# Seven products for the last column pairs of a down projection, on one core

## The chip, the cores and the metric

The kernel runs on one core of one Trainium2 chip. The metric is device time in microseconds (us): the median of three runs of the kernel before is 1959.01 us (1958.78 to 1959.5). One more execution was taken by the profiler; all lines of the profile and of the trace come from that one.

## The reference

The kernel computes an encoder trunk of two layers on 256 tokens of width 2048. Only the feed-forward part is touched by the change. Cut to that, the reference is:

```python
def conv_gated_ffn(h, w_up, conv_w, conv_b, w_down):
    a = depthwise_conv_centred(h @ w_up, conv_w, conv_b)
    g, u = jnp.split(a, 2, axis=-1)
    return (jax.nn.silu(g) * u) @ w_down
...
for l in range(DEPTH):
    ...                                   # norm, input projection, attention, gating, output projection
    x = x + conv_gated_ffn(rms_norm(x, norm2_g[l]), w_up[l], conv_w[l], conv_b[l], w_down[l])
```

`w_down[l]` has 5632 rows (44 row blocks of 128) and 2048 columns (4 column blocks of 512). The 256 tokens are two token blocks of 128, called m = 0 and m = 1.

## The kernel before

**Three products for one.** All arithmetic is float32 accurate, made from a faster format. Each operand is split into a high part (rounded, by ScalarE, here ACT) and a low part (the rest, a subtraction on VectorE, here DVE). A plain product of one row block, one column block and one token block takes three matmuls on TensorE (here PE): activation high with weight high, activation low with weight high, activation high with weight low. Each has a 128x128 stationary operand and 512 columns.

**Halves, pairs and pieces.** The feed-forward part runs in two halves of the hidden width: 20 row blocks, then 24 (`HALVES`). A half first makes its activations (`gate_and_up`, which fills `ys`), then multiplies them with `w_down`, in two groups ("pairs") of two column blocks: columns 0 and 1, then 2 and 3 (the loop over `group`, L1014). `down_blocks` lists the pieces of a pair in order. A plain piece is one column block with four row blocks (sometimes two): one load of 1 MB, one high part, one low part, 24 matmuls (`direct`, L221).

**Pieces by seven products.** Some pieces take two neighbouring row blocks and both column blocks of the pair, with the two token blocks: a 2x2 by 2x2 block product, which `seven` (L258) makes with seven products in place of eight, so with 21 matmuls in place of 24. It has a price on the other engines. DVE forms four sums of weight tiles (L268 to L270) in a second raw buffer, and both the weights (three tiles) and the sums (four tiles) are split (L264, L271, L272, L273). On the activation side `mixed` (L249) forms four sums of activation tiles on DVE and `parts` (L378) splits them; this is done once for a row pair and kept in `mixes`. Four extra accumulators take the shared products. When the pair's last such piece is done, `seven_out` (L308) adds them into the residual `xr` with one ACT copy and seven DVE operations, three of which (L318 to L320) have no urgency.

**Which pieces.** Before, `FAST` gives the first row block of each such pair of row blocks: three of ten in both pairs of the first half, four of twelve in the first pair of the second half, none in the second pair of the second half. There the order is by columns: all six pieces of column block 2, then all six of column block 3. `AFTER` says after how many plain pieces each stands.

**Buffers.** Raw weights have four buffers of 1 MB; a plain piece takes one, a piece by seven takes two. The high and low parts have three "wide" places each (`wide`, L149); a plain piece takes one, a piece by seven two. The input projections use the first two thirds of the same room as four "narrow" places of 1024 columns (`narrow`, L143). PSUM has three two-bank tiles `mm` and two one-bank tiles `tp`. A pair takes two `mm` for its sums, and with pieces by seven one more `mm` and both `tp`; in the very last pair of the last layer column block 3 has the two `tp` for its sums.

**Order.** Every engine's list is made by a scheduler from priorities: weight loads, splits and everything within `urgent()` come early, the rest fills in. `let_in` (L196), called in the middle of each piece, lets waiting steps in.

**Hand-over between layers.** When a column block c is finished in the first layer's second half, `done` adds it into `xr` (`residual`, L695), and `next_rows` (L651) makes the next layer's activations out of it: two ACT copies (L656), four transposing DMAs issued from SyncE (SP, L663), two ACT copies (L670) and four splits (L366 on ACT, L367 on DVE). The next layer's input projection reads them in order of c: it takes key block 0, 1, 2 (column blocks 0, 1, 2), then query block 0, then key block 3 (column block 3), each with 24 matmuls (L210, L215).

Of the kernel before, what the change touches and what calls it, by code (L numbers as in the profile page):

```python
# [15 lines left out]
P = 128  # L16
# [11 lines left out]
W = 512  # L28
KB = 4
# [4 lines left out]


HALVES = ((0, 20), (20, NF))
FAST = ((4, 8, 12), (4, 8, 12, 16))
AFTER = (2, 4, 5, 6)
PLACES = 6


def sevens(half, pair):

    return FAST[half] if half == 0 or pair == 0 else ()


def down_blocks(half, pair):

    f0, f1 = HALVES[half]
    c = (2 * pair, 2 * pair + 1)  # L50
    fast = sevens(half, pair)
    if not fast:
        return [((n,), tuple(range(k, min(k + KB, f1))), False) for n in c for k in range(f0, f1, KB)]
    plain = [k for k in range(f0, f1) if k - f0 - (k - f0) % 2 not in fast]
    own = [((n,), tuple(plain[i : i + KB]), False) for i in range(0, len(plain), KB) for n in c]
    for i, k in enumerate(fast):
        own.insert(AFTER[i] + i, (c, (f0 + k, f0 + k + 1), True))
    return own


# [7 lines left out]
def encoder(ctx: ExitStack, tc: tile.TileContext, xT, x, w_in, w_gu, w_o, w_up, w_down, wsT, pcol, prow, rope, out):  # L68
# [27 lines left out]
    def mm():  # L96
        return mmp.tile([P, 2, W], F32, tag="mm", name="mm")

    def tp(shape):
        return tpp.tile(shape, F32, tag="tp", name="tp")  # L100
# [603 lines left out]
    for l in range(DEPTH):  # L704
# [40 lines left out]
        for m in range(2):  # L745
            t = sl([P, W])
# [48 lines left out]
        for i in range(2):  # L795
# [5 lines left out]
            for m in range(2):  # L801
                t = row()
# [147 lines left out]
        def gate_and_up(j, ys, mixes):  # L950
            gs = []

            def gate_in(tall):
                for i in range(2):
                    g = together(tall[i])
                    y = convolved(g, 4 * j + 2 * i)
                    nc.scalar.activation(y, y, AF.Silu)
                    gs.append(y)

            def up_in(tall):  # L960
                for i in range(2):
                    u = together(tall[i])
                    y = gs[i]
                    t = convolved(u, NF + 4 * j + 2 * i)
                    nc.vector.tensor_tensor(out=y, in0=y, in1=t, op=ALU.mult)  # L965
                    for k in range(2):
                        ys.append(split_plain(y[:, k, :]))
                    k = len(ys) - 2
                    if k in FAST[half]:
                        e = mixed(y)  # L970
                        waiting.append(lambda e=e, k=k: mixes.__setitem__(k, parts(e, [P, W])))

            if j == 0:
                pss = [mm(), mm()]
                for b in range(NB):
                    for n in range(2):
                        up_rows(pss[n], n, j, b)
                        if b == NB - 1:
                            leave(pss[n], (gate_in, up_in)[n], 2)
                return  # L980
            for n in range(2):
                ps = mm()
                for b in range(NB):
                    up_rows(ps, n, j, b)
                leave(ps, (gate_in, up_in)[n], 2 + (j == f1 // 4 - 1))

        w_at = 0
        for half, (f0, f1) in enumerate(HALVES):
# [23 lines left out]
                        (nc.scalar if end and a else nc.sync).dma_start(out[:, m, c * W + a : c * W + a + step], to)  # L1012

            for group in range(2):  # L1014
                fast = sevens(half, group)
                blocks = down_blocks(half, group)
                sums, fresh = {}, {}
                n_fast = 0
                for n, (cs, ks, sevenfold) in enumerate(blocks):
                    end = last and not more and cs[0] == 3  # L1020
                    for c in cs:
                        if c not in sums:
                            t = None if end else mm()
                            sums[c] = [tp([P, W]) for _ in range(2)] if end else [t[:, m, :] for m in range(2)]
                            fresh[c] = set()
                    src = w_down[l, :, w_at : w_at + len(cs) * len(ks) * W]
                    w_at += len(cs) * len(ks) * W
                    acts = [ys[k - f0] for k in ks]
                    if sevenfold:
                        if n_fast == 0:  # L1030
                            t = mm()
                            extra = [t[:, 0, :], t[:, 1, :], tp([P, W]), tp([P, W])]
                        seven(
                            sums[cs[0]], sums[cs[1]], extra, acts, mixes[ks[0] - f0], src,
                            fresh[cs[0]], fresh[cs[1]], n_fast == 0, n_fast == len(fast) - 1,
                        )
                        n_fast += 1
                        if n_fast == len(fast):
                            seven_out(extra, cs[0])
                        continue  # L1040
                    c = cs[0]
                    finished = not any(c in b[0] for b in blocks[n + 1 :])
                    direct(sums[c], acts, src, fresh[c], finished, end and finished)
                    if finished:
                        done(c, sums[c], end)
# [71 lines left out]
```

## Time and profile before

| what | value |
| --- | --- |
| median of three runs | 1959.01 us |
| the profiled execution's own time | 1959.16 us |
| its span in the trace | 1957.4 us |
| time around the span | 1.76 us |
| granted TensorE clock over the span | 1.000 |
| matmuls | 8820 |
| weights read by the down projection in pieces of 1 MB / of 0.5 MB | 84 / 8 |

A stage in the trace is given by its start and end in us from the span's start. In this profile the start of a matmul in the chain that ended last lies some 0.16 us behind the start in the timeline; both are used as they stand. The layers' down projections lie here: first layer, first half 487.47 to 539.83 (columns 0 and 1) and 539.83 to 592.19 (columns 2 and 3); second half 853.31 to 915.87 and 915.87 to 981.15. Second layer: 1460.05 to 1512.41, 1512.41 to 1564.77, 1825.89 to 1888.45 and 1888.45 to 1953.74.

### The profile page before, as it was taken

The page shows a single profiled execution, that of the slowest core. Times are in us where ns is not written, and L with a number is a line of the kernel's source. Part 1 is how long each engine was busy: PE and PEld are TensorE (multiplying, and loading weights), DVE is VectorE, ACT ScalarE, POOL GpSimd, SP SyncE. Part 2 cuts the span into 40 slices and gives each one's busy share as a digit, 9 for nine tenths or more (in the row PEclk, how much of TensorE's full clock was granted, in tenths as well). Part 3 has the DMA queues.
Part 4 walks back from the last instruction along what each step waited for, and adds up shares of the span by engine and source line. Part 5 has one row for each costly group of instructions (what it writes and reads, how often), then busy time and mean ns, then how long its engine had stood idle before and what let it go on. Part 6 is the DMA issues. An engine that isn't in the chain of part 4 may idle for free.

```text
span 1957.4 us, 23117 instructions
## 1 busy us (share of the span) xinstructions
PE 1950.2 (100%) x8820; PEld 1619.1 (83%) x8820; DVE 1353.4 (69%) x1672; ACT 1326.1 (68%) x1461; POOL 21.3 (1%) x25
## 2 busy tenths in 40 slices
PE   9999999999999999999999999999999999999999
PEld 7888888888888888888888888888888888888887
DVE  5859775667875666678567796756669756666773
ACT  6776486777745777776566864877876556777742
POOL 0100000000000000000000000000000000000000
PEclk9999999999999999999999999999999999999999
DMA  9754586776566776657667446867765667677572
GB/s 360 217 199 151 195 256 192 218 226 215 185 219 219 222 222 214 221 164 269 196 202 249 143 163 213 247 199 223 227 212 186 220 212 228 210 224 225 163 269 85
DMA packets 191311, 414.04 MB, mean 212 GB/s; under 512 B 139488, under 2 KB 140768, under 8 KB 146656
## 3 DMA queue, kind: packets, MB, share of 16 engines
q1 hardware_dynamic: 190480, 411.83, 65.1%
q8 instruction: 69, 1.13, 0.2%
q10 hardware_dynamic: 720, 0.73, 0.1%
q14 instruction: 42, 0.34, 0.1%
HBM read 378.43 MB, written 2.10 MB: 194 GB/s over the span
## 4 chain that ended last, share of the span: by engine, by line
PE 97%; DMA 1%; DVE 1%; issue 0%; SPq 0%; ACT 0%; POOL 0%; DVEq 0%; ACTq 0%
PE mm L228 66%; PE mm L210 12%; PE mm L215 6%; PE mm L343 3%; PE tp L228 2%; PE mm L348 2%; PE mm L288 1%; PE mm L294 1%; PE mm L289 1%; DMA raw<-in_w_in 1%; DMA qk<-in_prow 1%; PE tp L289 0%; PE tp L294 0%; PE tp L288 0%; PE tp L386 0%; PE tp L616 0%
## 5 line engine op out<-in xcount | busy, mean ns | idle before, releaser
L156 DVE TENSOR_TENSOR los<-raw,his 128x2048 fp32r<-128x2048 f32 (+3 forms) x468 | 851.9, 1828 | 504.6 <-ACT his L182 362.5
L228 PE MATMUL mm<-his,sl 128*128 128x512 f32 x3808 | 902.4, 389 | 0.0
L228 PEld LDWEIGHTS mm<-his,sl 128*128 128x128 f32 x3808 | 715.0, 188 | 148.2
L182 ACT ACTIVATE his<-raw 128x2048 fp32r<-128x2048 f32 x248 | 466.8, 1883 | 182.9 <-PE mm L228 150.8
L228 PE MATMUL mm<-los,sl 128*128 128x512 f32 x1904 | 470.8, 389 | 0.0
L228 PEld LDWEIGHTS mm<-los,sl 128*128 128x128 f32 x1904 | 357.5, 188 | 74.1
L210 PE MATMUL mm<-his,sl 128*128 128x512 f32 x1152 | 311.0, 391 | 0.6 <-ACT his L171 0.5
L171 ACT ACTIVATE his<-raw 128x1024 fp32r<-128x1024 f32 (+1 forms) x180 | 186.0, 1039 | 158.5 <-PE mm L210 126.5
L210 PEld LDWEIGHTS mm<-his,sl 128*128 128x128 f32 x1152 | 215.1, 188 | 46.0 <-ACT his L171 0.9
L513 ACT COPY sl<-sl 128x1024 uint16<-128x1024 uint16 x98 | 132.3, 1350 | 112.8 <-DMA sl<-sl 112.8
L215 PE MATMUL mm<-los,sl 128*128 128x512 f32 x576 | 178.3, 390 | 1.2 <-DVE los L156 1.2
L215 PEld LDWEIGHTS mm<-los,sl 128*128 128x128 f32 x576 | 107.9, 188 | 24.3 <-DVE los L156 2.0
L916 ACT ACTIVATE sl<-sl,pc 128x256 f32<-128x256 f32 x176 | 95.3, 589 | 0.9
L937 ACT COPY sl<-sl 128x1024 uint16<-128x1024 uint16 x88 | 92.1, 1046 | 2.7
L917 DVE SCALAR_TENSOR_TENSOR sl<-sl,pc 128x255 f32<-128x255 f32 x176 | 77.4, 479 | 4.7 <-ACT sl L916 4.2
L920 DVE SCALAR_TENSOR_TENSOR sl<-sl,pc 128x255 f32<-128x255 f32 x176 | 77.4, 478 | 0.1
L374 ACT ACTIVATE sl<-sl 128x256 fp32r<-128x256 f32 x88 | 31.8, 408 | 66.1 <-DVE sl L965 66.1
L935 ACT ACTIVATE sl<-mm,yr 128x512 f32<-128x512 f32 x88 | 59.7, 679 | 4.9 <-PE mm L228 4.9
L343 PE MATMUL mm<-sl,his 128*128 128x512 f32 x256 | 62.1, 392 | 0.0
L271 ACT ACTIVATE his<-raw 128x2048 fp32r<-128x2048 f32 x20 | 38.3, 1913 | 28.6 <-DVE raw L270 26.6
L343 PEld LDWEIGHTS mm<-sl,his 128*128 128x128 f32 x256 | 47.1, 188 | 9.1
L367 DVE SCALAR_TENSOR_TENSOR sl<-sl,pc 128x256 fp32r<-128x256 f32 x96 | 42.2, 480 | 11.1 <-ACT sl L366 11.0
(145 smaller groups left out, 1167.5 us busy)
## 6 DMA issues: line engine op xcount, KB each, us to landing
raw<-in_w_up SPq DMA_DIRECT2D x176, 1024.0 KB, 5.0
raw<-in_w_down SPq DMA_DIRECT2D x84, 1024.0 KB, 4.6
raw<-in_w_in SPq DMA_DIRECT2D x38, 1024.0 KB, 5.0
raw<-in_w_o SPq DMA_DIRECT2D x32, 1024.0 KB, 4.9
raw<-in_w_gu SPq DMA_DIRECT2D x16, 1024.0 KB, 5.5
raw<-in_w_down SPq DMA_DIRECT2D x8, 512.0 KB, 3.3
sl<-sl SPq DMA_TRANSPOSE x244, 4.1
sl<-in_prow SPq DMA_DIRECT2D x12, 256.0 KB, 7.6
```

The lines of the kernel that those rows point to most:

```text
L156: nc.vector.tensor_tensor(out=lo, in0=part, in1=hi.bitcast(F32), op=ALU.subtract)
L171: nc.scalar.activation(hi[:, cs], part, AF.Copy)
L182: nc.scalar.activation(hi[:, :n], raw[:, :n], AF.Copy)
L210: nc.tensor.matmul(ps[m], acts[kk][:, part, m * P : (m + 1) * P], hi, start=first and kk == 0 and part == 0, stop=False,)
L215: nc.tensor.matmul(ps[m], acts[kk][:, 0, m * P : (m + 1) * P], lo, start=False, stop=last and kk == KB - 1)
L228: nc.tensor.matmul(ps[m], acts[kk][:, part % 2, m * P : (m + 1) * P], w, start=first, stop=done and kk == len(acts) - 1 and part == 2,)
L343: nc.tensor.matmul(ps[:, i, :], part_of(0, k, i), x1, start=k == 0, stop=False)
L513: nc.scalar.copy(words, tall.rearrange("p (b a) n -> p b (a n)", b=2))
L916: nc.scalar.activation(t[:, i, :], s[:, i, :], AF.Identity, bias=col(3), scale=col(1))
L917: nc.vector.scalar_tensor_tensor(out=t[:, i, 1:], in0=s[:, i, : SEQ - 1], scalar=col(0), in1=t[:, i, 1:], op0=ALU.mult, op1=ALU.add)
L920: nc.vector.scalar_tensor_tensor(out=t[:, i, : SEQ - 1], in0=s[:, i, 1:], scalar=col(2), in1=t[:, i, : SEQ - 1], op0=ALU.mult, op1=ALU.add)
L937: nc.scalar.copy(h, rows.bitcast(U16).rearrange("p (j n b) -> p j b n", j=2, b=2))
```

## The change

`FAST` and `AFTER` are given for each half and each pair. The second half's second pair now has four row pairs of twelve by seven products, placed as in its first pair; the first half's second pair has four of ten, one after each of the first four plain pieces. Its plain pieces are then six of four row blocks, where there were six of four and two of two. The row pair at block 16 of the first half gets its mixed activations, which it had not before. In the very last pair the four extra accumulators are two `mm` tiles, since column block 3 holds the two `tp`. The plain pieces of columns 2 and 3 in the second half now alternate, so that column block 2 ends one piece before column block 3. The weights are packed on the host in the new order of pieces.

```diff
 HALVES = ((0, 20), (20, NF))
-FAST = ((4, 8, 12), (4, 8, 12, 16))
-AFTER = (2, 4, 5, 6)
+FAST = (((4, 8, 12), (4, 8, 12, 16)), ((4, 8, 12, 16), (4, 8, 12, 16)))
+AFTER = (((2, 4, 5), (1, 2, 3, 4)), ((2, 4, 5, 6), (2, 4, 5, 6)))
...
-def sevens(half, pair):
-
-    return FAST[half] if half == 0 or pair == 0 else ()
...
-    fast = sevens(half, pair)
-    if not fast:
-        return [((n,), tuple(range(k, min(k + KB, f1))), False) for n in c for k in range(f0, f1, KB)]
+    fast = FAST[half][pair]
     plain = [k for k in range(f0, f1) if k - f0 - (k - f0) % 2 not in fast]
     own = [((n,), tuple(plain[i : i + KB]), False) for i in range(0, len(plain), KB) for n in c]
     for i, k in enumerate(fast):
-        own.insert(AFTER[i] + i, (c, (f0 + k, f0 + k + 1), True))
+        own.insert(AFTER[half][pair][i] + i, (c, (f0 + k, f0 + k + 1), True))
     return own
...
-                    if k in FAST[half]:
+                    if k in FAST[half][0] + FAST[half][1]:
                         e = mixed(y)
...
-                fast = sevens(half, group)
+                fast = FAST[half][group]
...
                         if n_fast == 0:
                             t = mm()
-                            extra = [t[:, 0, :], t[:, 1, :], tp([P, W]), tp([P, W])]
+                            extra = [t[:, 0, :], t[:, 1, :]]
+                            if last and not more and group:
+                                t = mm()
+                                extra += [t[:, 0, :], t[:, 1, :]]
+                            else:
+                                extra += [tp([P, W]), tp([P, W])]
```

## The prediction

> **What bounds the kernel now.** I read the page's first and fourth part, then the list of waits for PE, then the chain that ended last in order of time.
>
> ```profile
> span 1957.4 us, 23117 instructions
> PE 1950.2 (100%) x8820; PEld 1619.1 (83%) x8820; DVE 1353.4 (69%) x1672; ACT 1326.1 (68%) x1461; POOL 21.3 (1%) x25
> ...
> PE 97%; DMA 1%; DVE 1%; issue 0%; SPq 0%; ACT 0%; POOL 0%; DVEq 0%; ACTq 0%
> ```
>
> The chain is PE work for 97% of the span. A busy PE is no proof of a full one, so the waits come next (engine and line that waited, whom for: us in total, times, longest).
>
> ```profile
> PE mm L215 <- DVE los L156: 1.2, 1, 1.2
> PE tp L124 <- DVE ones L120: 1.1, 1, 1.1
> PE tp L616 <- DVE sl L608: 0.5, 1, 0.5
> PE mm L210 <- ACT his L171: 0.5, 1, 0.5
> ```
>
> That is the whole list: 3.3 us, none of it on a line of the down projection (L228 and L288 to L294). The chain gives the pace (start, length, matmuls).
>
> ```profile
> 269.87 228.48 PE mm L228 x1008
> ...
> 884.59 5.44 PE mm L228 x24
> 894.79 5.44 PE mm L228 x24
> 904.99 76.16 PE mm L228 x336
> ...
> 1877.57 43.52 PE mm L228 x192
> 1921.09 32.65 PE tp L228 x144
> ```
>
> 228.48 / 1008 = 0.22667 us a matmul. The same pace stands in 5.44 / 24 and 76.16 / 336. Between the two pieces of 24 lies a piece by seven: 894.79 - 884.59 - 5.44 = 4.76 us, and 21 x 0.22667 = 4.76. So a piece by seven runs at the plain pace too, and is 0.68 us shorter than the 24 matmuls that it replaces, with no wait before, in or behind it. PE is the bound here, and matmuls taken away come off the end one for one, as long as the others keep up.
>
> **The change part by part.** *Matmuls removed.* In a layer the first half's second pair goes from 231 to 228 (one more piece by seven), the second half's second pair from 288 to 276 (four more). That is 15 a layer, 30 in all: 30 x 0.22667 = **6.80 us**. The removed matmuls lie in the four stages that follow (the stage, then its length, busy us and number of instructions of PE, PEld, DVE, ACT, POOL, the granted clock, the DMA share, GB/s); the third row is the second half's first pair, which already has four of twelve.
>
> ```profile
> 487.47:539.83 52.36, 52.36 (x232) 43.37 (x232) 46.27 (x52) 37.71 (x37) 0.00 (x0) 1.00 0.56 194
> 539.83:592.19 52.36, 52.36 (x232) 43.37 (x232) 42.01 (x34) 24.35 (x16) 0.00 (x0) 1.00 0.62 218
> 853.31:915.87 62.56, 62.56 (x277) 51.82 (x277) 54.71 (x56) 43.67 (x39) 0.00 (x0) 1.00 0.64 227
> 915.87:981.15 65.28, 65.28 (x289) 54.07 (x289) 34.00 (x30) 43.72 (x50) 0.00 (x0) 1.00 0.63 206
> 1888.45:1953.74 65.29, 65.28 (x289) 53.73 (x287) 26.48 (x16) 17.40 (x10) 0.00 (x0) 1.00 0.38 132
> ```
>
> Here a rule speaks about the size of the gain. The Trainium skill, "TensorE: Matmul & The Clock Gate", section "Back-to-back issue gap", gives about 131 ns as the sustained spacing of 512-column matmuls in a real kernel, and N/2.4 + 2.5 ns, some 216 ns, for an isolated warm one. As estimates from that page the sum would be 30 x 0.131 = 3.9 us or 30 x 0.216 = 6.5 us. This trace has neither (0.22667 us over 1008 in a row), and the row decides.
>
> *DVE work added.* The prices (busy us, mean ns of one):
>
> ```profile
> L156 DVE TENSOR_TENSOR los<-raw,his 128x2048 fp32r<-128x2048 f32 x12 | 27.4, 2289 | 7.7 <-ACT his L271 7.2 <-ACT his L182 0.5
> L156 DVE TENSOR_TENSOR los<-raw,his 128x1536 fp32r<-128x1536 f32 x4 | 7.0, 1754 | 2.6 <-PE mm L228 2.6
> L268 DVE TENSOR_TENSOR raw<-raw 128x1024 f32<-128x1024 f32 x3 | 3.7, 1222 | 0.0
> ...
> L269 DVE TENSOR_TENSOR raw<-raw 128x512 f32<-128x512 f32 x3 | 2.1, 685 | 0.0
> ...
> L320 DVE TENSOR_TENSOR xr<-xr,sl 128x1024 f32<-128x1024 f32 x1 | 1.2, 1214 | 0.0
> ```
>
> A plain piece costs DVE 2.29 us, one by seven 1.22 + 2 x 0.69 + 1.75 + 2.29 = 6.64, so 4.35 more. `seven_out` is six operations of L269's size and one L320: 6 x 0.69 + 1.21 = 5.3. For the first layer's last pair that makes 34.00 + 4 x 4.35 + 5.3 = 56.7 us in a stage of 65.28 - 2.72 = 62.56, a share of 91%; for the second layer's 26.48 + 22.7 = 49.2, 79%. In the first half's second pair one piece by seven stands for two half pieces: at most 42.01 + 6.64 = 48.7 in 51.68, 94%, less what the two half pieces cost. The stages that run without a wait today have 54.71 / 62.56 = 87% and 46.27 / 52.36 = 88%. So DVE stays under PE in each stage, but with little left. I take 0, and keep 0 to 2 us in all for sevens whose low parts come late by the bunching of this work. ACT has more room:
>
> ```profile
> L264 ACT ACTIVATE his<-raw 128x1536 fp32r<-128x1536 f32 x20 | 29.8, 1489 | 19.3 <-PE mm L228 12.2 <-PE mm L289 7.0
> ```
>
> A piece by seven splits three tiles more than a plain one, 1.49 us; four make 43.72 + 6.0 = 49.7 of 62.56 in the first layer's last pair, 79%. Cost 0.
>
> *The mixed activations of block 16 in the first half* are new:
>
> ```profile
> L253 DVE TENSOR_TENSOR sl<-sl 128x256 f32<-128x256 f32 x14 | 5.9, 418 | 0.0
> L254 DVE TENSOR_TENSOR sl<-sl 128x128 f32<-128x128 f32 x14 | 4.1, 292 | 0.5
> L381 DVE TENSOR_TENSOR sl<-sl 128x512 fp32r<-128x512 f32 (+1 forms) x28 | 18.1, 652 | 25.2 <-ACT sl L380 25.2
> ```
>
> 0.42 + 2 x 0.29 + 0.65 = 1.65 us of DVE, in the stage of 46.27, which goes to 47.9 of 52.36. They are read only in the next stage. Cost 0, cover: those 4.5 us.
>
> *The first piece by seven of the first half's second pair* comes one plain piece earlier, and after a pair's end, where DVE also adds the sums into `xr`:
>
> ```profile
> 545.64 1.92 ACT L271 ACTIVATE his<-raw 128x2048 fp32r<-128x2048 f32 x1 [5.14 <-DVE raw L270]
> ...
> 550.71 0.23 PE mm L288
> ```
>
> Today its sums are split from 545.64 to 547.56. It would start at 550.71 - 5.44 = 545.27 and needs them nine matmuls in, at 547.31. Kept at its present time the split would hold PE for 0.25 us; but the second plain piece's low part now comes behind it in the order, which gives back up to 2.29 us. I take 0, bounds 0 to 0.3 in each layer.
>
> *Loads.* Eight half loads turn into four whole ones, the bytes are the same. A piece by seven holds two of four raw buffers; the alternation of the third stage row does so already without a wait. I take 0.
>
> *The hand-over between the layers* is the step without a direct row. Column block 2 used to end 32.64 us before column block 3, now 5.44. Call the end of column block 3 E. The next layer needs block 2's first activations behind two key blocks, at E + 2 x 24 x 0.22667 = E + 10.88. What the chain behind a finished column block takes, from the addition to the first split activation, is bounded by three pairs of rows, an L695 and an L367 (of whose two or four operations the first is ready some 0.45 us in):
>
> ```profile
> 912.81 0.68 DVE L318 TENSOR_TENSOR xr<-xr,sl 128x512 f32<-128x512 f32 x1
> ...
> 914.02 1.28 DVE L695 TENSOR_TENSOR xr<-mm,xr 128x512 f32<-128x512 f32 x2
> ...
> 929.57 1.67 DVE L367 SCALAR_TENSOR_TENSOR sl<-sl,pc 128x256 fp32r<-128x256 f32 x4
> ...
> 948.54 1.29 DVE L695 TENSOR_TENSOR xr<-mm,xr 128x512 f32<-128x512 f32 x2 [3.01 <-PE mm L228]
> ...
> 956.75 0.89 DVE L367 SCALAR_TENSOR_TENSOR sl<-sl,pc 128x256 fp32r<-128x256 f32 x2
> ...
> 981.48 1.28 DVE L695 TENSOR_TENSOR xr<-mm,xr 128x512 f32<-128x512 f32 x2
> ...
> 992.16 0.88 DVE L367 SCALAR_TENSOR_TENSOR sl<-sl,pc 128x256 fp32r<-128x256 f32 x2 [0.91 <-ACT sl L366]
> ```
>
> Block 2 today takes 956.75 + 0.45 - 948.54 = 8.7 us, block 3 11.1, block 0, which today stands just as block 2 will (after a `seven_out`, one piece before its neighbour), 16.0. When the addition can start is the second unknown. Block 0 ended at 904.99 + 5.44 = 910.43 and was added only from 914.02, 3.6 us later, because L318 and L319, without urgency, waited behind low parts; block 3, with no `seven_out` before it, 0.3 later. So block 2's first activations come between E - 5.1 + 8.7 = E + 3.6 and E - 1.9 + 16.0 = E + 14.1, and the wait is 0 to 3.2 us. The nearest row for the chain is block 3's 11.1, the same engines at the same place, and with the late start it gives E + 9.2: in time by 1.7 us. Block 0's 16.0 had no date to keep. I take 0. On SP the two sets of four transposes now stand 5.4 us apart:
>
> ```profile
> 984.34 5.23 SPq L663 DMA_TRANSPOSE sl<-sl  x4
> ```
>
> During each, SP issues no load for 5.2 us, and PE lives on the pieces already loaded; blocks 0 and 1 did the same to the pair behind them, without a wait. Block 3's own activations are due at E + 21.8; with 2.7 for the start and 16.0 for the chain they come at 18.7.
>
> *The end.* Block 2 of the last layer is written out one piece before the end, not six; nothing follows that would fill DVE, so I take 0 (0 to 0.6).
>
> **The sum** is 6.80: span 1957.4 to 1950.6. The profiled execution took 1959.16, so 1.76 lies around the span, and 0.15 over the median of 1959.01. Against the median the forecast is **1952.2 us**.
>
> **The rivals.** *The hand-over waits.* Block 2's chain goes like block 0's: PE waits at key block 2, up to 3.2 us once. For it: block 0 stands the same way; against it: block 3's chain beside the same input projection. Time 1952.5 to 1955.4. *DVE falls behind* in the dense stages: up to 2 us, 1952.5 to 1954.5, for it the 91%, against it that 87% and 88% run with no wait at all. *Slower than before:* the transposes of block 2 stand in SP's list behind a weight load that waits for a raw buffer.
>
> ```profile
> SPq L164 <- DVE los L156: 376.8, 73, 17.6
> ```
>
> SP has waited up to 17.6 us at such a load. Behind that one, activations due at E + 10.9 come at E + 9.2 + 17.6 = 26.8: a wait of 15.9, 9.1 over the gain, 1968.1 us. It decides from a wait of 6.8 on, and shows as slower from 10.7. Against it: the mean of those 73 waits is 5.2 us, which with 1.7 us of room leaves 3.5. The Trainium skill, the same page, section "What's actually happening", halves PE's clock after an idle window of about 3.4 us; by it such a wait would also cost some matmuls double. No wait here is that long (the list above), and every stage row has the clock at 1.00, so no run shows it. *A removed matmul gives back less than its pace*, as by the spacing of 131 ns in that page: 3.9 us, 1955.1; the rows speak against it. That the pieces by seven are not made is out: the lists are plain.
>
> **How the numbers follow.** Forecast without new waits 55%; hand-over 27%, of which 4 with more than 2.9 us; DVE late 9%, of which 2 come together with a hand-over wait and pass 2.9; SP's order 4%, of which 3 past 10.7 us; the smaller gain 1%; 4% for a better time by up to 1.3 us, since a new order also moves the 3.3 us of waits elsewhere. About 0.2%, 3.9 us, is what a measurement here tells from no change: faster means below 1955.1. Faster 55 + 23 + 7 + 4 = 89%, within 4 + 2 + 1 + 1 = 8%, slower 3%. The range is 1951.2 to 1955.5: below, part of the better case; above, the whole of the hand-over's bound.
>
> **What would show it.** Right: the chain shows all thirty pieces by seven of the two layers at 4.76 us; 8790 matmuls; no wait of PE between 487 and 592 or 853 and 1010. The hand-over wrong: PE waits on L366 or L367 at key block 2, some 10.9 us behind the last L228 of the first layer. DVE wrong: PE waits on L156 at L294. SP wrong: L663 stands behind a long wait of L164. The forecast is wrong, too, if attention in the second layer, where PE waits a little already, is ordered anew.

## The result, and the profile after

| | median, us | lowest to highest | runs |
| --- | --- | --- | --- |
| before | 1959.05 | 1958.78 to 1960.86 | 8 |
| after | 1954.23 | 1953.08 to 1956.62 | 8 |

The ratio is 0.9975, with a 95% interval of 0.9964 to 0.9986. The change makes the kernel faster by 4.8 us, of the 6.8 that were forecast. The forecast of 1952.2 is 2.0 too low, and the time lies inside the range.

In the changed kernel the lines behind `sevens` stand seven lower: L228 is now L221 (plain matmuls), L288 to L294 are L281 to L287 (pieces by seven), L268 to L270 are L261 to L263 (sums of weight tiles), L271 is L264 (high part of the sums), L210 and L215 are L203 and L208 (input projection), L171 and L182 are L164 and L175 (high parts of its weights and of plain pieces), L156 is L149 (low parts), L695 is L688 (addition), L663 and L670 are L656 and L663 (transposes, and the copies behind them), L366 and L367 are L359 and L360 (first split activations). L426 are the squares of a finished column block. Some experiments have one or two lines more: in e6 and e10, for example, the addition is L689.

These lines of the page of the kernel after answer to those shown of before: the span, the busy times, the chain by engine.

```profile
span 1953.7 us, 23130 instructions
...
PE 1946.0 (100%) x8790; PEld 1614.0 (83%) x8790; DVE 1404.9 (72%) x1732; ACT 1340.8 (69%) x1473; POOL 21.3 (1%) x25
...
PE 97%; DVE 1%; ACT 0%; issue 0%; POOL 0%; DVEq 0%
```

There are 8790 matmuls, 30 fewer, and PE is still the bound. The list of waits for PE has one entry that was not there before:

```profile
PE mm L203 <- DVE sl L360: 1.4, 2, 1.2
```

It is two waits. The long one, 1.15 us, ends at 30.11 us, in the start of the program, which the change doesn't touch (e1 comes back to it). The short one, 0.24 us, ends at 991.38, at key block 2 of the second layer.

To see what the change gave, I cut the run by the chain that ended last. Its longest pieces begin at fixed places of the program: the 1008 matmuls begin with the first half's up projection, the 1248 with the last 48 matmuls ahead of the second half's. After:

```profile
271.83 228.48 PE mm L221 x1008
...
582.91 282.88 PE mm L221 x1248
...
1242.07 228.48 PE mm L221 x1008
...
1553.16 282.88 PE mm L221 x1248
...
1944.85 5.45 PE tp L221 x24
```

Before, those not shown yet:

```profile
581.31 282.88 PE mm L228 x1248
...
1242.45 228.48 PE mm L228 x1008
...
1553.89 282.88 PE mm L228 x1248
```

| stretch (start to start) | before | removed, x 0.22667 | would be | after | lost |
| --- | --- | --- | --- | --- | --- |
| start to first up projection | 269.87 | 0 | | 271.83 | (see e1) |
| first half, layer 1 | 311.44 | 3: 0.68 | 310.76 | 311.08 | 0.32 |
| second half, hand-over, attention | 661.14 | 12: 2.72 | 658.42 | 659.16 | 0.74 |
| first half, layer 2 | 311.44 | 3: 0.68 | 310.76 | 311.09 | 0.33 |
| second half, layer 2, to the last matmul | 399.85 | 12: 2.72 | 397.13 | 397.14 | 0.01 |
| first up projection to last matmul | 1683.87 | 6.80 | 1677.07 | 1678.47 | 1.40 |

The last row is the work that the change touches: 5.40 us less, 1.40 lost, in two places. The first is the hand-over. Here the chain itself leaves PE (start, length, what):

```profile
986.38 0.43 PE mm L208 x2
986.81 0.70 ACT sl L426 x3
987.52 1.24 ACT sl L663
988.75 0.93 ACT his L164
...
989.71 1.23 DVE los L149
990.93 0.41 DVE sl L360
...
991.38 0.97 PE mm L203 x3
```

The chain before the change was all matmuls at this place. Now it goes through ACT: two squares of another block (L426), the copy behind a transpose (L663), a split of a weight, a low part, and only then the activation that PE waits for. With E the end of column block 3 (980.03), the first L360 is done at 991.28, E + 11.25, and it was due at about E + 10.88. The list's 0.24 us are only a part of what this costs. By the starts of successive matmuls PE loses 0.40 us at the one that waits for the first L360 and 0.11 at the next, and 0.23 more twelve matmuls on, at the second L360: 0.74, all that the stretch lost.

The second place is the last piece by seven of the first half's first pair, whose matmuls the change doesn't touch. Timeline after (start, length, engine and line, in brackets the idle time before):

```profile
521.58 0.75 DVE L368 TENSOR_TENSOR sl<-sl 128x256 fp32r<-128x256 f32 x2
522.25 0.69 DVE L374 TENSOR_TENSOR sl<-sl 128x512 fp32r<-128x512 f32 x1
522.85 0.69 DVE L262 TENSOR_TENSOR raw<-raw 128x512 f32<-128x512 f32 x1
523.46 1.75 DVE L149 TENSOR_TENSOR los<-raw,his 128x1536 fp32r<-128x1536 f32 x1
...
524.43 1.92 ACT L175 ACTIVATE his<-raw 128x2048 fp32r<-128x2048 f32 x1 [2.61 <-issue]
525.12 0.69 DVE L263 TENSOR_TENSOR raw<-raw 128x512 f32<-128x512 f32 x1
...
526.25 1.90 ACT L264 ACTIVATE his<-raw 128x2048 fp32r<-128x2048 f32 x1
...
527.35 0.84 PE L287 MATMUL mm<-los,sl 128*128 128x512 f32 x3
...
528.20 0.50 PE L281 MATMUL mm<-his,sl 128*128 128x512 f32 x1
```

Ahead of the sums L262 and L263 DVE splits activations (L368) and a mixed activation (L374). L263 ends late, at 525.81, and by then ACT is splitting a plain piece (L175, to 526.35), so that L264 starts only at 526.25. In the kernel before, in e4 and in e5 that plain split stands behind the split of the sums. L264 ends at 528.15, and PE's tenth matmul starts at 528.20, not at 527.35 + 3 x 0.22667 = 528.03. The list of waits doesn't have this one. It shows only in the starts of successive matmuls, 0.17 late here and 0.11 more at the next (528.54).

### The profile page after: what moved, and what is told of

Same layout as the page of the kernel before. It is cut to its first block, busy times and chain, and to the rows that moved or that the text cites. A ratio compares the mean times of both kernels' runs of the same rounds, so it can differ in the third digit from the quotient of the medians.

```text
span 1953.7 us, 23130 instructions
## 1 busy us (share of the span) xinstructions
PE 1946.0 (100%) x8790; PEld 1614.0 (83%) x8790; DVE 1404.9 (72%) x1732; ACT 1340.8 (69%) x1473; POOL 21.3 (1%) x25
## 4 chain that ended last, share of the span: by engine, by line
PE 97%; DVE 1%; ACT 0%; issue 0%; POOL 0%; DVEq 0%
PE mm L221 64%; PE mm L203 12%; PE mm L208 6%; PE mm L336 3%; PE mm L281 2%; PE mm L282 2%; PE mm L287 2%; PE mm L341 2%; PE tp L221 1%; PE tp L287 1%; PE tp L282 1%; PE tp L281 1%; PE tp L379 0%; PE tp L609 0%; PE tp L380 0%; PE tp L381 0%
## 5 line engine op out<-in xcount | busy, mean ns | idle before, releaser
L149 DVE TENSOR_TENSOR los<-raw,his 128x2048 fp32r<-128x2048 f32 (+3 forms) x476 | 867.6, 1833 | 466.3 <-ACT his L175 321.4
L221 PE MATMUL mm<-his,sl 128*128 128x512 f32 x3680 | 872.1, 389 | 0.0
L221 PEld LDWEIGHTS mm<-his,sl 128*128 128x128 f32 x3680 | 690.9, 188 | 143.2
L175 ACT ACTIVATE his<-raw 128x2048 fp32r<-128x2048 f32 (+1 forms) x236 | 446.8, 1895 | 123.0 <-PE mm L221 97.5
L221 PE MATMUL mm<-los,sl 128*128 128x512 f32 x1840 | 454.7, 389 | 0.0
L221 PEld LDWEIGHTS mm<-los,sl 128*128 128x128 f32 x1840 | 345.5, 188 | 71.6
L203 PE MATMUL mm<-his,sl 128*128 128x512 f32 x1152 | 312.2, 392 | 1.4 <-DVE sl L360 1.4
L164 ACT ACTIVATE his<-raw 128x1024 fp32r<-128x1024 f32 (+1 forms) x180 | 186.2, 1039 | 146.7 <-PE mm L203 125.5
L203 PEld LDWEIGHTS mm<-his,sl 128*128 128x128 f32 x1152 | 215.4, 188 | 47.7 <-DVE sl L360 2.9
L208 PE MATMUL mm<-los,sl 128*128 128x512 f32 x576 | 178.4, 390 | 1.2 <-DVE los L149 1.2
L208 PEld LDWEIGHTS mm<-los,sl 128*128 128x128 f32 x576 | 107.9, 188 | 24.4 <-DVE los L149 2.0
L264 ACT ACTIVATE his<-raw 128x2048 fp32r<-128x2048 f32 x30 | 57.4, 1914 | 63.9 <-DVE raw L263 38.6
L367 ACT ACTIVATE sl<-sl 128x256 fp32r<-128x256 f32 x88 | 31.9, 409 | 70.4 <-DVE sl L958 70.4
L257 ACT ACTIVATE his<-raw 128x1536 fp32r<-128x1536 f32 x30 | 44.6, 1487 | 28.7 <-PE mm L221 19.1
L281 PE MATMUL mm<-his,sl 128*128 128x512 f32 x154 | 60.1, 390 | 0.0
```

What stands on the lines that cost most here:

```text
L149: nc.vector.tensor_tensor(out=lo, in0=part, in1=hi.bitcast(F32), op=ALU.subtract)
L164: nc.scalar.activation(hi[:, cs], part, AF.Copy)
L175: nc.scalar.activation(hi[:, :n], raw[:, :n], AF.Copy)
L203: nc.tensor.matmul(ps[m], acts[kk][:, part, m * P : (m + 1) * P], hi, start=first and kk == 0 and part == 0, stop=False,)
L208: nc.tensor.matmul(ps[m], acts[kk][:, 0, m * P : (m + 1) * P], lo, start=False, stop=last and kk == KB - 1)
L221: nc.tensor.matmul(ps[m], acts[kk][:, part % 2, m * P : (m + 1) * P], w, start=first, stop=done and kk == len(acts) - 1 and part == 2,)
```

## The experiments

The same kernel's time differs by 3.5 us from run to run (the table above), more than most parts of this question are worth. So each experiment is read by the stretches of its trace as in the table; e1 shows how well these repeat. "Full" is the third column of numbers: 310.76, 658.42, 310.76, 397.13.

| run | median, us | ratio to before, interval | first half 1 | second half to next | first half 2 | second half 2 | sum |
| --- | --- | --- | --- | --- | --- | --- | --- |
| e1_again | 1953.68 | 0.9974 [0.9964, 0.9985] | 311.07 | 659.11 | 311.08 | 397.13 | 1678.39 |
| e2_only_second | 1954.49 | 0.9976 [0.9967, 0.9986] | 311.44 | 659.50 | 311.44 | 397.13 | 1679.51 |
| e3_only_first | 1958.28 | 0.9996 [0.9987, 1.0005] | 311.09 | 661.10 | 311.10 | 399.85 | 1683.14 |
| e8_order_alone | 1959.7 | 1.0002 [0.9993, 1.001] | 311.44 | 661.06 | 311.44 | 399.85 | 1683.79 |
| e4_early_mix | 1953.16 | 0.9972 [0.9961, 0.9982] | 311.05 | 659.14 | 311.03 | 397.14 | 1678.36 |
| e5_raw5 | 1952.97 | 0.997 [0.9958, 0.9981] | 310.76 | 659.15 | 310.76 | 397.13 | 1677.80 |
| e10_lo_later | 1955.17 | 0.9981 [0.9972, 0.999] | 311.59 | 659.18 | 311.59 | 397.13 | 1679.49 |
| e6_urgent_out | 1954.2 | 0.9975 [0.9966, 0.9984] | 311.60 | 659.12 | 311.51 | 397.15 | 1679.38 |
| e7_col2_earlier | 1952.68 | 0.9969 [0.9957, 0.998] | 311.16 | 658.41 | 311.08 | 397.13 | 1677.78 |
| e9_squares_dve | 1953.5 | 0.9972 [0.9961, 0.9982] | 311.13 | 658.41 | 311.10 | 397.13 | 1677.77 |
| e11_both | 1952.69 | 0.9969 [0.9957, 0.9981] | 310.76 | 658.35 | 310.76 | 397.12 | 1676.99 |
| e12_more | 1951.95 | 0.9965 [0.9952, 0.9977] | 310.08 | 658.37 | 310.08 | 397.13 | 1675.66 |

### e1: the changed kernel once more

No edit.

> The changed kernel once more, to separate what the change does from what a run does. The measure is the stretch from the first matmul of the first layer's up projection to the last matmul: 1683.87 us before, 1678.47 in the changed kernel's profile, 5.40 less (6.80 for 30 matmuls, less waits of some 0.33 in each layer's first half and 0.74 around the hand-over). Theory A (the first 272 us differ from run to run, whatever the change): the stretch is again 1678.5 within 0.2, and the start of the up projection lies anywhere from 269.9 to 272. Theory B (the change makes the start late): it starts at 271.8 again, within 0.2, in this and every other variant, and the kernel before stays near 269.9.

The four stretches repeat within 0.05 us. What doesn't repeat is the start: the first up projection begins at 269.88 us here, at 271.83 in the first trace, with the same program. One DVE operation near the start, first in e1:

```profile
25.95 0.17 DVE L473 TENSOR_SCALAR nsink<-qk 128x8 f32<-128x8 f32 x1 [3.63 <-DMA qk<-in_prow]
```

and the same one, with what follows it, in the first trace of the changed kernel:

```profile
28.33 0.17 DVE L473 TENSOR_SCALAR nsink<-qk 128x8 f32<-128x8 f32 x1 [5.70 <-DMA qk<-in_prow]
...
29.58 0.48 DVE L360 SCALAR_TENSOR_TENSOR sl<-sl,pc 128x256 fp32r<-128x256 f32 x1
...
30.11 0.98 PE L203 MATMUL mm<-his,sl 128*128 128x512 f32 x3 [1.15 <-DVE sl L360]
```

DVE's list holds a small operation (L473) that waits for a load of 132 KB, and the activation for which PE waits (L360) stands behind it. In the first trace the load landed 2.4 us later than in e1, and PE stood still. This is also the 1.2 us in the list of waits above. So the traced run of the changed kernel shows 1.95 us more than e1 for a reason that has nothing to do with the change.

### e2, e3, e8: the parts one by one

e2 keeps the first half as before and makes only the second half's second pair by sevens; e3 does the opposite; e8 makes no new piece by seven and only alternates the plain pieces of columns 2 and 3.

```diff
 # e2
-FAST = (((4, 8, 12), (4, 8, 12, 16)), ((4, 8, 12, 16), (4, 8, 12, 16)))
-AFTER = (((2, 4, 5), (1, 2, 3, 4)), ((2, 4, 5, 6), (2, 4, 5, 6)))
+FAST = (((4, 8, 12), (4, 8, 12)), ((4, 8, 12, 16), (4, 8, 12, 16)))
+AFTER = (((2, 4, 5), (2, 4, 5)), ((2, 4, 5, 6), (2, 4, 5, 6)))
 # e3 (with the old order by columns where there are no sevens)
+FAST = (((4, 8, 12), (4, 8, 12, 16)), ((4, 8, 12, 16), ()))
 # e8
+FAST = (((4, 8, 12), (4, 8, 12)), ((4, 8, 12, 16), ()))
```

> Only the second half's second pair by seven products; the first half as before. 24 matmuls less, 5.44 us. Theory A (the wait of 0.33 in each layer's first half comes from the new mixed activations of block 16, and the 0.74 from the hand-over): stretch 1683.87 - 5.44 + 0.7 = 1679.1, no wait in the first half, the hand-over wait as in the changed kernel. Theory C (the first-half wait comes from something else in the new order): the first half is 0.3 longer here too, stretch 1679.8.

> Only the first half's second pair with four of ten; the second half's second pair plain and by columns as before. 6 matmuls less, 1.36 us. Theory A: less two waits of 0.33: stretch 1683.87 - 1.36 + 0.66 = 1683.2, no wait at the hand-over. If the 0.74 is not of the hand-over but of a shifted schedule in the second layer, it is here as well: 1683.9.

> The kernel before with one thing of the change: the plain pieces of the second half's second pair alternate between columns 2 and 3, with no piece by seven there. Same matmuls as before. Theory A (order and seven_out make the hand-over late together): without a seven_out block 2 is added at once, some 5.1 us before the layer's end, and its first activations come with 8.7 to 11.1 us of chain at 3.6 to 6.0 us behind the end, due at 10.9: no wait, 661.1 us. Rival (the nearness of the two hand-overs alone does it): 661.8.

The parts add up but for one thing. e2 saves 1683.87 - 1679.51 = 4.36, e3 0.73, together 5.09; the whole saves 5.40 to 5.48. The rest of 0.3 to 0.4 is lost in e2's attention of the second layer, where its chain goes through a transfer that the chains before, after and of e1 don't have:

```profile
1091.14 6.61 DMA sl<-sl
```

The stretches tell more: the first half loses its 0.3 us only with the first half's part of the change (e1, e3), and the hand-over its 0.7 only with the second half's (e1, e2). e8 loses nothing: alternating the columns brings column block 2's end to 5.44 us before E, and the next layer still comes in time. With no `seven_out` ahead of it block 2 is added at E - 5.1 there, and the first L360 is done at E + 9.0, 1.8 us before its date. e8 beside before also says that the order by itself is worth nothing (1.0002 [0.9993, 1.001]).

### e4, e5, e10: what holds the first half

The suspects are the mixed activations of block 16 on DVE, the four raw buffers, and the order of DVE's list. e4 takes another row pair, block 2 in place of 16, whose activations are made earlier. e5 has a fifth raw buffer (with two small slots fewer, to have the room). e10 puts the low part of the three weight tiles behind the last sum.

```diff
 # e4
-FAST = (((4, 8, 12), (4, 8, 12, 16)), ...
+FAST = (((4, 8, 12), (2, 4, 8, 12)), ...
 # e5
-    slots = pool("slots", 54)
-    rawp = pool("rawp", 4)
+    slots = pool("slots", 52)
+    rawp = pool("rawp", 5)
 # e10
-            lo_part(lo[:, : 3 * W], raw[:, : 3 * W], hi[:, : 3 * W])
+            with tc.issue_after(latest(nc.vector.engine)):
+                lo_part(lo[:, : 3 * W], raw[:, : 3 * W], hi[:, : 3 * W])
```

> As the changed kernel, but the fourth row pair of the first half's second pair starts at block 2 instead of block 16, so that its mixed activations are made during the up projection and not in the crowded stage behind it. Same 30 matmuls less. Theory A: the first half's first pair is back at 52.36 us in both layers, stretch 1678.47 - 0.66 = 1677.8. Rival (the last piece by seven of the first pair waits because of the denser order behind it, whatever is mixed): the wait of 0.3 stays, stretch 1678.5.

In e4 the wait at the first pair's last piece by seven is gone, so the mixed activations in that stage brought it there. But the first half is as long as it was (311.05 against 311.08): the loss now stands at the *second* pair's last piece. The mixing decided where the time is lost, not whether. Timeline of e4:

```profile
578.59 4.49 DVE L149 TENSOR_TENSOR los<-raw,his 128x2048 fp32r<-128x2048 f32 x2 [2.06 <-ACT his L264]
...
580.93 0.50 PE L287 MATMUL mm<-los,sl 128*128 128x512 f32 x1
```

PE's L287 needs the low part of the sums, the first of the two L149, done at 578.59 + 2.29 = 580.88. The bracket tells why it is late: DVE stood still for 2.06 us until ACT had split the sums. The same stillness is in each turn of plain piece and piece by seven. One turn of DVE in the changed kernel:

```profile
561.88 1.22 DVE L261 TENSOR_TENSOR raw<-raw 128x1024 f32<-128x1024 f32 x1
563.01 1.75 DVE L149 TENSOR_TENSOR los<-raw,his 128x1536 fp32r<-128x1536 f32 x1
564.68 0.68 DVE L262 TENSOR_TENSOR raw<-raw 128x512 f32<-128x512 f32 x1
565.40 0.69 DVE L263 TENSOR_TENSOR raw<-raw 128x512 f32<-128x512 f32 x1
568.16 4.49 DVE L149 TENSOR_TENSOR los<-raw,his 128x2048 fp32r<-128x2048 f32 x2 [2.06 <-ACT his L264]
572.57 1.22 DVE L261 TENSOR_TENSOR raw<-raw 128x1024 f32<-128x1024 f32 x1
```

From L261 to L261 a turn takes 572.57 - 561.88 = 10.69 us, of which DVE works 8.6. PE's turn is 5.44 + 4.76 = 10.20. So in the alternation DVE loses 0.49 us a turn to PE, however idle it is on average, and lives on the lead with which it enters.

> The changed kernel with five raw buffers instead of four (and 52 small slots instead of 54, to make room). In the first half's second pair, where plain pieces and pieces by seven alternate, DVE's first sum (L261) comes every 10.69 us, while PE needs 4.76 + 5.44 = 10.20 us for the two pieces: 0.49 us of the lead is lost in each turn. Theory D (the loop of 10.69 us closes through the raw buffers): with a fifth the sums come earlier, the period is 10.20 or less, and the first half is 310.76 long in both layers instead of 311.08. Theory E (the loop is DVE's list itself, which waits 2.06 us for ACT's L264 in each turn, whatever the buffers): the period stays 10.69 us, and the first half 311.08. The hand-over keeps its 0.7 in both.

e5 has the full length, 310.76 in both layers. The period is the other theory's: two successive L261 of e5 are still 10.69 apart.

```profile
558.06 1.22 DVE L261 TENSOR_TENSOR raw<-raw 128x1024 f32<-128x1024 f32 x1
...
568.75 1.22 DVE L261 TENSOR_TENSOR raw<-raw 128x1024 f32<-128x1024 f32 x1
```

So the fifth buffer doesn't shorten the turn. It lets DVE and ACT enter the alternation earlier: the last L261 comes 568.75 - 269.53 = 299.2 us behind the first up projection, against 572.57 - 271.83 = 300.7 in the changed kernel. Those 1.5 us are more than the 0.3 that were lost. (e5 has two small slots fewer as well; no run has the fifth buffer without that.)

> The changed kernel with one edge in seven: the low part of the three weight tiles is put behind the third sum (L263) in DVE's list, so that it fills the wait for ACT's L264. A fifth raw buffer had left the period of L261 at 10.69 us. Theory E (the loop of 10.69 us is DVE's list): 1.7 of the 2.06 us of waiting are filled, the loop could close in some 9.0 us, so the period becomes PE's 10.20 us; the sums of every piece by seven are ready earlier, so the wait of 0.33 at the first pair's last piece goes too: first half 310.76 in both layers, hand-over still 659.1. If the period stays above 10.20, another loop (raw buffers) is behind it, and the first half is 311.08 or longer.

e10 does shorten the turn. Timeline of e10:

```profile
546.06 1.28 DVE L689 TENSOR_TENSOR xr<-mm,xr 128x512 f32<-128x512 f32 x2
...
547.39 0.50 PE L282 MATMUL mm<-his,sl 128*128 128x512 f32 x1 [0.53 <-DVE xr L689]
...
559.42 1.22 DVE L261 TENSOR_TENSOR raw<-raw 128x1024 f32<-128x1024 f32 x1
...
569.62 1.22 DVE L261 TENSOR_TENSOR raw<-raw 128x1024 f32<-128x1024 f32 x1
```

A turn is 10.20, PE's own pace, and the waits for the sums are gone. But the kernel is slower than the changed one, by 0.5 us in each first half: a new wait of 0.8 us in all (0.68 and 0.11 in the starts) stands at the second pair's first piece by seven. There PE wants the PSUM tile that the addition of the column before (L689) still reads, and this addition now stands one low part further back in DVE's list. That is the place for which the prediction had bounds of 0 to 0.3 us a layer.

### e6, e7, e9: what holds the hand-over

e6 makes the last three additions of `seven_out` urgent, so that column block 2 is added earlier. e7 lets column block 2 end one place earlier. e9 leaves all times of the additions as they are and puts only the squares of column blocks 2 and 3 on DVE.

```diff
 # e6, around the three additions
+        with urgent():
             nc.vector.tensor_tensor(out=xr[:, 0, l], in0=xr[:, 0, l], in1=t, op=ALU.add)
 ...
 # e7
-AFTER = (..., ((2, 4, 5, 6), (2, 4, 5, 6)))
+AFTER = (..., ((2, 4, 5, 6), (2, 3, 4, 5)))
+    if half and pair:
+        own[5], own[6] = own[6], own[5]
 # e9
-                        sum_squares(ssq, c)
+                        sum_squares(ssq, c, c >= 2)
```

> The changed kernel with the last three additions of seven_out (L311 to L313) urgent too, everywhere. Theory A (the hand-over wait comes from the late addition of block 2, which waits for L311 and L312 behind four low parts of the next layer's weights): the addition comes some 2 to 3 us earlier, the 0.7 us of waits at key block 2 are gone, and the stretch from the second up projection to the next layer's first is 661.14 - 2.72 = 658.4 instead of 659.1. Rival (the chain is held by ACT and by the transposes whenever it starts, or the earlier additions hold up low parts): 659.1 or more.

Timeline of e6, whose E is at 978.22:

```profile
974.01 1.28 DVE L689 TENSOR_TENSOR xr<-mm,xr 128x512 f32<-128x512 f32 x2
...
976.87 5.43 SPq L657 DMA_TRANSPOSE sl<-sl  x4
...
985.62 1.33 ACT L664 COPY sl<-sl 128x1024 uint16<-128x1024 uint16 x1
...
989.57 0.96 PE L203 MATMUL mm<-his,sl 128*128 128x512 f32 x3 [0.24 <-DVE sl L361]
```

The addition comes at E - 4.2, 2.3 us earlier than in the changed kernel (978.09, E - 1.9), and the transposes are issued from E - 1.4. The wait of PE is the same 0.24, and the copy behind the transposes starts at E + 7.40, in the changed kernel at 987.42, E + 7.39. An earlier addition buys nothing, because in ACT's list this copy stands behind the copies of column block 3, a split and two squares. The Trainium skill, "PSUM — Partial Sum Buffer", section "Engine vs sequencer instructions", calls the queues of ScalarE and VectorE strictly first in, first out; this trace agrees, with a copy that didn't move by 0.1 us when the addition at the head of its chain came 2.3 us earlier. So the early addition can't be what kept e8 in time. There ACT's list differs: block 3's first copy (L649) starts at E + 1.04, in the changed kernel at E + 3.32, where a split of the next layer's weights (L164, from E + 2.35) stands ahead of it; the copy behind the transposes follows at E + 5.15, against E + 7.39. e6 also takes 0.5 us more in each first half than the changed kernel. In layer 1 0.37 of it stands at the second pair's last piece by seven, as in e4; the earlier additions are the only edit, but how they cause it was not followed up.

> The changed kernel with the second half's second pair in another order: pieces by seven after 2, 3, 4 and 5 plain ones, then the last piece of column block 2, then two of column block 3, so that block 2 ends 10.88 us before the layer's end and not 5.44. Theory A: no wait at the hand-over, 658.4 us from up projection to up projection. The four pieces by seven now stand in three close turns; by the period of 10.69 against 10.20 they lose 1.5 us of lead, which shows as 0 to 0.4 us of wait at the last one in each layer.

e7's wait is gone: 658.41 is the full length. Its column block 2 is added 7.4 us before E, and here the whole chain moves with it, since its end no longer meets column block 3's. The 0 to 0.4 us that were allowed for the last of its four close pieces by seven didn't come: 397.13 in the second layer.

> The changed kernel with the sums of squares of column blocks 2 and 3 at the hand-over on DVE (L421) instead of ACT (L426). Making block 2's addition 2.3 us earlier left the start of ACT's first copy of the transposed block (L663) at 7.4 us behind the layer's end, behind block 3's copies, a split and two squares in ACT's list. Theory F (that list, not the addition, holds the chain): without the squares the first copy starts some 2 us earlier, and the 0.7 us of waits at key block 2 are gone: 658.4 us from the second up projection to the next layer's first instead of 659.1. Theory A (the addition): 659.1 still. The first half keeps its 311.08 in both.

Timeline of e9, whose E is at 979.11:

```profile
984.68 1.36 ACT L663 COPY sl<-sl 128x1024 uint16<-128x1024 uint16 x1 [0.27 <-DMA sl<-sl]
...
988.13 0.88 DVE L360 SCALAR_TENSOR_TENSOR sl<-sl,pc 128x256 fp32r<-128x256 f32 x2
```

The addition is where it was (E - 1.95). With the squares out of ACT's list the copy behind the transposes comes ahead of the split of the weight, and starts at E + 5.57, now waiting for its transfer. The first L360 is done at E + 9.5. That is in time by 1.4 us, and the stretch has its full length. So the 0.74 us came from the order of ACT's list, and taking the squares out of it is enough to save them.

### e11, e12: both remedies, and one step more

e11 is the changed kernel with the edits of e5 and e9. e12 is e11 with four pieces by seven in the first half's first pair too, both of its pairs taking blocks 2, 4, 8 and 12.

```diff
 # e12, beside the edits of e5 and e9
+FAST = (((2, 4, 8, 12), (2, 4, 8, 12)), ((4, 8, 12, 16), (4, 8, 12, 16)))
+AFTER = (((1, 2, 3, 4), (1, 2, 3, 4)), ((2, 4, 5, 6), (2, 4, 5, 6)))
```

> The change with both remedies together: the fifth raw buffer, and the squares of column blocks 2 and 3 at the hand-over on DVE. Theory: the two losses are independent, one in the first halves (0.32 us a layer, a lead of DVE that runs out), one at the hand-over (0.73 us, ACT's list). Then both go: first half 310.76 us in each layer, second half with hand-over and attention of the first layer 658.42, second half of the second layer 397.13, so 1677.07 from the first up projection to the last matmul, all 6.80 us that were predicted; with the start between 269.5 and 271.8 and 3.4 + 1.8 us behind, a time of 1951.8 to 1954.0. Rival: they are one effect of how DVE's and ACT's work is ordered and meet each other, so that the squares on DVE bring back part of the first loss or the fifth buffer part of the second: 1677.4 or more, with a wait of PE named in one of those places.

> e11 with one more piece by seven in each layer: the first pair of the first half takes four of ten as well, 3 matmuls fewer a layer. Theory that the pace of PE still bounds: first half 310.08 us in each layer, 1675.71 in all, 1.36 us less than e11. Rival, DVE's list bounds: that stage then holds four turns of plain piece and piece by seven, of 10.69 us on DVE against 10.20 on PE, a loss of 0.49 a turn, so up to 4 x 0.49 = 1.96 us a layer less the lead at its start; the gain of 0.68 a layer is eaten and the first half takes 310.5 us or more, with PE waiting on the sums of the last pieces by seven of each pair.

The first and the last of the long pieces of e11's chain:

```profile
270.18 228.48 PE mm L221 x1008
...
1941.72 5.45 PE tp L221 x24
```

1941.72 + 5.45 - 270.18 = 1676.99: all that was forecast, and 0.1 more. e12 takes 1.33 us off that again, where six matmuls are worth 1.36; no wait of PE is left in its first halves, and its rival fell. Its turn is still 10.69 in the second pair, so it too runs on the lead. Its ratio to before is 0.9965 [0.9952, 0.9977]. By the medians it is the fastest kernel of the study, though its interval and that of the changed kernel overlap; by its trace it has 1678.47 - 1675.66 = 2.8 us less between the first up projection and the last matmul.

## Why the prediction came out as it did

**Matmuls removed: right, and of the right size.** With the waits gone 30 matmuls are worth 6.88 us (e11; 0.07 of it lies in the stretch with the attention), for the 6.80 forecast; the second layer's second half gave 2.71 of 2.72 at once. The estimate of 3.9 us by the spacing of 131 ns in the Trainium skill ("TensorE: Matmul & The Clock Gate", "Back-to-back issue gap") does not hold for this kernel.

**DVE work added: the sums a little high, the reading of them wrong.** The windows of the first half's two pairs, first layer, and of the second half's second pair in both layers, after (stage, length, busy us of PE, PEld, DVE, ACT, POOL, clock, DMA share, GB/s):

```profile
489.43:542.11 52.68, 52.67 (x233) 43.24 (x232) 46.46 (x56) 37.05 (x37) 0.00 (x0) 1.00 0.57 193
542.11:593.79 51.68, 51.68 (x230) 42.81 (x229) 45.28 (x35) 26.93 (x16) 0.00 (x0) 1.00 0.59 225
...
917.47:980.03 62.56, 62.56 (x278) 51.82 (x277) 54.34 (x50) 43.75 (x44) 0.00 (x0) 1.00 0.72 234
...
1887.72:1950.28 62.56, 62.56 (x277) 51.48 (x275) 47.95 (x39) 24.26 (x14) 0.00 (x0) 1.00 0.43 154
```

DVE is busy for 54.34 us where 56.7 were worked out, 47.95 for 49.2, 45.28 for at most 48.7, 46.46 for 47.9. The one of these stages that lost time is the first row, 52.68 for 231 matmuls worth 52.36. Its DVE share is 88.2%, hardly more than the 87.6% of the second row, which lost nothing, and its matmuls aren't among those that changed.

**The step that failed first: DVE's work was taken as covered, "Cost 0, cover: those 4.5 us"** for the mixed activations of block 16, and 0 for low parts that come late by bunching. It cost 0.32 us in layer 1 and 0.33 in layer 2. The 4.5 us were the idle time of the whole stage; the work came in one place, between two sums that a piece by seven was waiting for. The bound of 0 to 2 us for bunching held it; the value of 0 didn't. The mixing alone isn't the price, since e4 moves it away and loses as much one stage later. Both places live on one lead: a turn of DVE takes 10.69 us, one of PE 10.20. Behind it stands the step on **loads**: "the alternation of the third stage row does so already without a wait" was true as an observation, but its reason wasn't the buffers, since e10 closes the turn in 10.20 us with four of them. The stage shown has two such turns in a row, the first half's second pair now three; whether the stage shown lives on a lead too was not measured.

**The first piece by seven of the second pair: right by a hair.** It cost nothing in the changed kernel. e10 shows what the place costs when one low part stands in front: 0.8 us, through the addition and its PSUM tile, not through the split that the prediction looked at.

**The step that failed second: the hand-over's 11.1 us.** The addition came at E - 1.94, as taken (E - 1.9). The chain behind it took 991.28 - 978.09 = 13.2, not block 3's 11.1, inside the bounds of 8.7 and 16.0. The row was the nearest in place, but block 3 had no other block's steps ahead of its own in ACT's list, and block 2 now has block 3's. So the rival to which I gave 27% happened, at 0.74 us of its 3.2, and at the place that the prediction named for it. SP's order, the third rival, didn't come into it: the transposes were issued at 979.88, while the copies that feed them still ran.

**The end: right.** 397.14 of 397.13.

**The sum.** The median of the eight runs lies 2.0 us over the forecast. With the seven runs of e1, which is the same program, the median of fifteen is 1953.68, 1.5 over, and 1.40 of that are the waits above. The rest is small beside what moves from run to run: the start, by up to 2.3 us (next but one section), and the time around the span, taken as 1.76 and here 1.75 to 2.92. The change doesn't make the start later on average: the median span of the fifteen runs is 1951.7, 5.5 less than the 1957.2 of the 24 runs of the kernel before that were taken beside e1, and the touched work alone is 5.40 to 5.48 shorter. Of the prediction's own signs, the 8790 matmuls came; "no wait of PE between 487 and 592 or 853 and 1010" didn't hold, at 528.20 and at 991.38.

## What to carry to other kernels

An engine's share of a stage says whether its work fits, not whether it comes in time: look at the turn of the loop in that stage, and compare the helper's period, with the waits in its own list, with the bound engine's (10.69 against 10.20 here). A helper that is slower per turn runs on lead, so a buffer more can pay without any shorter turn. When a step is moved beside another, its chain runs in one list with the other's: a chain measured alone can be too short (11.1 us against 13.2 here), and making its first step earlier is worth nothing if a later step stands behind the neighbour's.

## What the runs showed of the hardware that was not expected

**One late load moves the whole program.** All 14 traces of this study have L473 (in some under a neighbouring number), and the start of the first up projection goes with it:

| L473 starts at | 24.52 | 25.08 | 25.95 | 26.42 | 26.69 | 27.03 | 27.14 | 27.35 | 27.45 | 27.59 | 28.33 |
| --- | --- | --- | --- | --- | --- | --- | --- | --- | --- | --- | --- |
| up projection at | 269.56 | 269.50 | 269.88 | 269.87 | 270.18 | 270.56 | 270.62 | 270.86 | 270.98 | 271.08 | 271.83 |
| kernel | e2 | e6 | e1 | before | e11 | e10 | e7 | e9 | e8 | e4 | after |

The three left out (e3, e5, e12: 25.55 to 25.74) start at 269.52 to 269.90. From some 26.4 us on, a later landing costs as much as it is late (28.33 - 26.42 = 1.91, and 271.83 - 269.87 = 1.96); before that it costs nothing that shows, and the starts lie between 269.50 and 269.90 in no order of the landing. The kernel before and the one after both stand in this row, so it isn't the change. That moving the small operation back in DVE's list would take the spread away is only argued: it wasn't tried.

**Short waits are not in the list.** In the first half 0.28 us went between matmuls for which no idle time is recorded. Only the distance of their starts shows it. At the hand-over the list has 0.24 of 0.74 us.
